# A hybrid decoder step on one core: follow-up steps as streams of their own, decays and heads ahead of the searches, sample values in 128 rows

## The chip, the core and the metric

The kernel runs on one core of a Trainium2 chip. A core has a matrix engine (TensorE, PE in the profile; PEld is its weight load), a vector engine (VectorE, DVE), a scalar engine (ScalarE, ACT), a general engine (GpSimd, POOL) and a queue that issues most transfers (SyncE, SP). Each engine works off its own list of instructions in order; semaphores join them. The metric is the device time of one execution in microseconds (us), as the median of several runs.

## The reference

One layer of a decoder for 1024 prompt tokens and 64 sample tokens (8 sequences of 8), 1088 columns in all, with a model width of 1024:

```python
def token_mixer(x, ...):
    z = split_projection(x @ w_in)              # q_a k_a v_a q_i k_i w_i q_b k_b v_b g_b a_b gate_a gate_b
    attn = attend(q_a, k_a, v_a, q_i, k_i, z['w_i'])   # top 256 keys by an indexer, then softmax
    log_a = log_sigmoid(z['a_b'] @ w_alpha2 + b_alpha) / GATE_TAU
    o_b, s_new = gla_chunked(q_b, k_b, v_b, log_a, gla_s0, gla_chunk)
    o_b = o_b * rsqrt(mean(o_b * o_b) + eps) * gla_norm_g * silu(z['g_b'])
    merged = sigmoid(gate_a) * (attn @ w_attn_o) + sigmoid(gate_b) * (o_b @ w_gla_o)
    return merged @ w_out, k_a, v_a, k_i, s_new

def gla_chunked(...):    # per chunk, 4 heads, key width 128, value width 256
    q_t, k_t = qx * exp(cum), kx * exp(-cum)
    o = tril(q_t @ k_t.T) @ vx + q_t @ s
    s = exp(last) * s + (kx * exp(last - cum)).T @ vx

h = layer_norm(ALPHA * x + mix_out);  y = layer_norm(ALPHA * h + square(relu(h @ w_ff1)) @ w_ff2)
```

The indexer scores every key for every query (`relu(q_i k_i)`, weighted by `w_i`) and keeps the 256 best. For samples the keys are 4096 cached ones, spread over pages, and the new ones.

## The kernel before

Weights and activations are split into a high and a low part, and every projection runs as three matmuls per block of 128 inputs (high x high, low x high, high x low) over columns 0 to 384, 384 to 768 and 768 to 1088. `front` computes everything up to the merged branches and the output projection; `back` does the layer norms and the MLP (`pf`, about 40% of the matmul time).

**What sets the order.** The program is written out once, by a planner. A `Clock` keeps an estimated time for each engine, for each tile the time at which it is ready, and for buffers the time at which they come free. Steps of the work are generators, `Stream`s in a list; a generator yields the tiles that it needs next. `Order.run` takes the first stream of the list whose needs are met by the estimated time of PE (or, if none is, the one whose needs are met first) and lets it issue up to its next yield. So an earlier place in the list is a higher priority, and all steps between two yields go to the engines' lists together. `Engine` passes every instruction through one line, L256, which is why all rows of the profile name that line; they are told apart by their tiles.

**The streams that matter here.**
- `main` runs the jobs, one per block of 128 output columns: `misc` (small projections), `qi`, `ka`, `qa`, `qb`/`kb`, `vb` (`psv`), `gb` (the output gate of GLA), `gate`, then `pmb` (GLA output), `pma` (attention output) and `pwo`. `w_split` makes the high part `wh` of a weight on ACT and the low part `wl` on POOL or DVE.
- `top_first` and `top_second` search the threshold of the prompt's top 256 bit by bit (32 counting steps), on DVE (`ga`) and ACT with DVE (`gb`). Then `fin` turns each tile of scores into a mask (`gta`, `gtb`, `msk`).
- `top_sample` does the same for the samples: in each of 32 steps ACT counts over two halves (`jka`), PE adds the counts (`ppr`), DVE takes the bit (`gs_m`, `gs_u`) and sets the next threshold (`gs_f`).
- `decays` makes the decay factors of a GLA head (`psa`, `cu`, `ge`), `heads` runs the recurrence: `gla` goes through 8 chunks of 128 tokens and, in `sample`, updates the sample states (`pus`, `us`, `gst`) with sample values as a high part `gvh` (128 rows, the values twice) and a low part `gvl` (64 rows), while the keys `gkz` hold high and low parts in rows 0 to 63 and 64 to 127.
- `idx_prompt` and `idx_sample` score the keys (`rh`, `rl`); gathers `cig` fetch the cached indexer keys on POOL's queue.
- `at_soft` and `at_pv` are the attention: scores `psq`, weights `pp`, transposes `ppt`, their high and low parts `phl`, the product `pov`, the output `ao`/`ahl`, stored to `at_s`.
- `ob_load` and `ob_split` fetch the GLA output `ob_s` again as `obl` (eight blocks, first columns 0 to 384, then the other 704) and split it into `obh` and `obl`, which `pmb` multiplies. `gate_job` stores gates to `ga_s` and `gt_load` fetches them as `mgt`.
- `ln_last`, in `back`, is the layer norm of the last columns: sums over eight tiles on PE (`plv`, `pld`), then mean, root and reciprocal on columns of `lr`.

Of the kernel before, what the change touches and what calls it, by code (L numbers as in the profile page):

```python
# [23 lines left out]
P = 128  # L24
# [25 lines left out]
NSH = 6  # L50
# [9 lines left out]
NAHL = 4  # L60
# [314 lines left out]
def front(ph, tc, env, A, O):  # L375
# [37 lines left out]

    def scale_rows(x, r):
# [25 lines left out]
    def w_split(i):  # L440
        for n, e in enumerate(wt[i]):
# [4 lines left out]
            sub(l, r, f32(h), WLATE if 1 < state["job"] < mix_at - 1 else 0.0)  # L446
            e[0], e[1] = h, l

    state = {"dma": 0, "split": 0, "job": 0}

    def w_get(i):
# [6 lines left out]
        hs, ls = [], []  # L458
        for h, l, kn in wt.pop(i):
            for k in range(kn):  # L460
                hs.append(h[:, k, :])
                ls.append(l[:, k, :])
# [182 lines left out]
    def to_stacks(ps, c, st):  # L645
# [5 lines left out]
        for e in range(2):  # L651
            own, oth = slice(e * 64, e * 64 + 64), slice(64 - e * 64, 128 - e * 64)
            dve.tensor_sub(st[e][oth, c0:c0 + n], ps[own, :n], f32(st[e][own, c0:c0 + n]))
# [4 lines left out]
    def qi_job(f):  # L658
        def run(w):
            st = [page(f"qi{2 * f + e}", F32R) for e in range(2)]  # L660
            for c in range(3):
                ps = yield from fmajor(w, c, f"qi{f}_{c}")
                to_stacks(ps, c, st)
# [31 lines left out]
    def qa_job(f):  # L695
        def run(w):
            st = [page(f"qa{2 * f + e}", F32R) for e in range(2)]
            for c in range(3):
                ps = yield from fmajor(w, c, f"qa{f}_{c}")
                to_stacks(ps, c, st)  # L700
# [55 lines left out]
    def idx_sample():  # L756
# [30 lines left out]
        def chunk(p, kh, kl, n):  # L787
# [7 lines left out]
            dve.scalar_tensor_tensor(rl[:, :n], ps[:, :n], 0.0, f32(rh[:, :n]), op0=OP.max, op1=OP.subtract)  # L795
            return rh, rl

        def sums(p, r, n, po, first, last):
            rh, rl = r
# [4 lines left out]
        for qq in range(4):  # L804
            po = [bank("po0", True), bank("po1", True)]
            pend = None
            for p in range(4):
# [7 lines left out]
                for e in range(2):  # L815
# [3 lines left out]
                    if pend:  # L819
                        yield [pend[1][1]]  # L820
                        sums(*pend)
                    pend = (p, r, 512, po[e], p == 0, p == 3)
            yield [pend[1][1]]
# [8 lines left out]
        for p in range(4):  # L832
            r = chunk(p, kkn[:, 0], kkn[:, 1], 64)
            yield [r[1][:, :64]]
# [140 lines left out]
    def masks(g, qts, gte):  # L975
        for i, grp in enumerate(MKP if not mk else ()):
# [207 lines left out]
    def gla(h):  # L1184
# [17 lines left out]
        dve.tensor_sub(vl[:TS], vs[:TS], f32(vh[:TS]))  # L1202
        qz = small("gqz", 512).rearrange("p (a b) -> p a b", b=TS)
# [8 lines left out]
        def sample():  # L1212
# [4 lines left out]
            for i in range(2):  # L1217
# [8 lines left out]
                for j in range(2):  # L1226
                    yield [kz, vh, vl[:TS]]
                    pu = bank("pus")
                    for x in range(2):
                        pe.matmul(pu[:, x * 256:(x + 1) * 256], kz[:, 2 * j + x, :], vh, start=True, stop=False)  # L1230
                        pe.matmul(pu[:, x * 256:(x + 1) * 256], kz[:TS, 2 * j + x, :], vl[:TS], start=False, stop=True)
                    for x in range(2):
                        b = 2 * j + x
                        la = g["lasts"][:, 4 * i + b:4 * i + b + 1]
                        u = small("us", 256)
# [6 lines left out]
            act.activation(vs[:TS], po[:TS, :256], AF.Copy)  # L1242

# [21 lines left out]
        for ci in range(8):  # L1265
# [20 lines left out]
            else:  # L1286
                S2 = small("S", 256)
                dve.scalar_tensor_tensor(S2, S, g["last"][:, ci:ci + 1], u, op0=OP.mult, op1=OP.add)
                S = S2
            if ci < 7:  # L1290
                Sm = small("Sm", 256)
                act.activation(Sm, S, AF.Copy, scale=g["mid"][:, ci + 1:ci + 2])
# [26 lines left out]

    def g_job(h, j):  # L1320
        def run(w):
# [3 lines left out]
            for c in range(3):  # L1325
                c0, n = CH[c]
                pg = yield from fmajor(w, c, f"gb{h}{j}_{c}")
                t = small("gt")
# [53 lines left out]
    def at_soft():  # L1382
# [7 lines left out]
        def norm(x):  # L1390
            rc = tiny("rc", 1)
            dve.reciprocal(rc, x[3][:, 3:4])
            scale_rows(x[2][:, :(x[0][0] + 1) * P], rc)
# [6 lines left out]
        for i, (qt, hp) in enumerate(units):  # L1400
# [11 lines left out]
            for h in range(2):  # L1412
# [18 lines left out]
                if len(fly) > 2:  # L1431
                    yield [fly[0][3][:, 3:4]]
                    norm(fly.popleft())
            if i == len(units) - 1:
                yield [fly[-1][3][:, 2:3]]
                expo(fly[-1])
                while fly:
                    yield [fly[0][3][:, 3:4]]
                    norm(fly.popleft())

    def at_pv():
        tails = deque()

        def tail(qt, hp, po):
# [4 lines left out]
            act.activation(t[:64], po[64:128], AF.Copy)  # L1449
            dve.tensor_tensor(o[:64], po[0:64], t[:64], op=OP.add)  # L1450
# [3 lines left out]
            act.activation(hl[0:64], o[:64], AF.Copy)  # L1454
            sub(hl[64:128], o[:64], f32(hl[0:64]))
            yield [hl]
            c, x0 = qt // 3, (qt % 3) * P
            for e in range(2):
                sp.dma_start(view(f32(at_s[c]), 2 * hp * 64 * 768 + e * 384 + x0, [[768, 64], [64 * 768, 2], [1, P]]),
                             f32(hl[e * 64:e * 64 + 64].rearrange("p (h q) -> p h q", q=P)))  # L1460

# [6 lines left out]
        for _ in units:  # L1468
# [11 lines left out]
            for kt in range(0, qt + 1, 2):  # L1480
# [11 lines left out]
                if len(pend) > 1:  # L1492
                    yield [pend[0][2]]
                    flush(*pend.popleft(), False)
# [5 lines left out]
            while pend:  # L1500
                yield [pend[0][2]]
                flush(*pend.popleft(), not pend)
# [52 lines left out]
    def ob_load():  # L1555
        yield lambda: state["job"] >= merge_at - OBLEAD
# [192 lines left out]
def back(ph, tc, env, A, O):  # L1749
# [114 lines left out]
    def ln(c, z, s, gi, emit, tag):  # L1864
# [28 lines left out]
        r3 = clock.take(pgs.tile([P, 4], F32, name="lr", tag="r3", bufs=2), "lr", "r3", 2)  # L1893
# [633 lines left out]
```

## Time and profile before

| | us |
|---|---|
| median of 3 runs (lowest to highest) | 2090.97 (2090.45 to 2092.82) |
| profiled execution, its own time | 2094.44 |
| its span | 2092.7 |
| PE busy | 2039.7 (97%) |
| DVE busy | 1261.8 (60%) |
| ACT busy | 1121.3 (54%) |
| POOL busy | 774.9 (37%) |
| mean granted clock of PE | 0.987 |

Times in rows of the profile are from the start of the span. Matmuls are pipelined: a row's duration is longer than the distance to the next start, so it is the distance that a matmul costs. A wait is put down to the semaphore that came last.

### The profile page before, as it was taken

The page shows a single profiled execution, that of the slowest core. Times are in us where ns is not written, and L with a number is a line of the kernel's source. Part 1 is how long each engine was busy: PE and PEld are TensorE (multiplying, and loading weights), DVE is VectorE, ACT ScalarE, POOL GpSimd, SP SyncE. Part 2 cuts the span into 40 slices and gives each one's busy share as a digit, 9 for nine tenths or more (in the row PEclk, how much of TensorE's full clock was granted, in tenths as well). Part 3 has the DMA queues.
Part 4 walks back from the last instruction along what each step waited for, and adds up shares of the span by engine and source line. Part 5 has one row for each costly group of instructions (what it writes and reads, how often), then busy time and mean ns, then how long its engine had stood idle before and what let it go on. Part 6 is the DMA issues. An engine that isn't in the chain of part 4 may idle for free.

```text
span 2092.7 us, 34594 instructions
## 1 busy us (share of the span) xinstructions
PE 2039.7 (97%) x12443; PEld 1965.4 (94%) x12443; DVE 1261.8 (60%) x2630; ACT 1121.3 (54%) x2222; POOL 774.9 (37%) x579
## 2 busy tenths in 40 slices
PE   7999999999799999999999999999999999999998
PEld 7989999898789999999999899999899999999997
DVE  6976776756845666753167844565654453566635
ACT  5678777787567765674023424455353242445543
POOL 3344121212221113113134324565655343354455
PEclk9999999999899999999999999999999999999998
DMA  6664301212023224245473234655533343235542
GB/s 237 260 188 140 124 21 51 95 34 92 23 72 127 83 83 139 84 135 196 170 277 121 71 89 130 188 155 166 148 100 111 122 130 107 66 129 163 186 151 89
DMA packets 185596, 264.51 MB, mean 126 GB/s; under 512 B 22208, under 2 KB 119488, under 8 KB 185424
## 3 DMA queue, kind: packets, MB, share of 16 engines
q1 hardware_dynamic: 177872, 236.87, 35.1%
q0 software_dynamic: 7552, 25.43, 3.9%
q8 instruction: 98, 1.61, 0.3%
q14 instruction: 74, 0.61, 0.1%
HBM read 212.72 MB, written 49.51 MB: 125 GB/s over the span
## 4 chain that ended last, share of the span: by engine, by line
PE 87%; DVE 5%; issue 4%; POOL 2%; ACT 2%; DMA 1%; SPq 0%; ACTq 0%; POOLq 0%; DVEq 0%
PE pf L256 32%; PE gate L256 9%; PE gb L256 5%; PE pwo L256 4%; PE psv L256 4%; PE pmb L256 4%; PE qb L256 2%; PE kb L256 2%; PE qa L256 2%; PE po L256 2%; PE qi L256 2%; PE psc L256 2%; PE pma L256 2%; PE psq L256 2%; PE pov L256 2%
## 5 line engine op out<-in xcount | busy, mean ns | idle before, releaser
L256 PE MATMUL pf<-a,w 128*128 128x384 f32 (+1 forms) x2304 | 397.4, 328 | 2.3 <-POOL a L256 1.3
L256 PE MATMUL pf<-h,w 128*128 128x384 f32 (+1 forms) x2304 | 396.4, 329 | 3.0 <-POOL w L256 1.7
L256 PEld LDWEIGHTS pf<-h,w 128*128 128x128 f32 x2304 | 380.9, 189 | 5.6 <-POOL w L256 2.1
L256 PEld LDWEIGHTS pf<-a,w 128*128 128x128 f32 x2304 | 378.4, 188 | 6.6 <-POOL a L256 1.8
L256 POOL TENSOR_TENSOR wl<-wr,wh 128x1024 fp32r<-128x1024 f32 (+1 forms) x66 | 150.6, 2283 | 470.0 <-ACT wh L256 415.1
L256 POOL TENSOR_TENSOR w<-wr,w 128x512 fp32r<-128x512 f32 x142 | 202.2, 1433 | 130.6 <-ACT w L256 122.0
L256 ACT ACTIVATE w<-wr 128x512 fp32r<-128x512 f32 x272 | 156.5, 618 | 62.2 <-PE pwo L256 25.8
L256 DVE TENSOR_TENSOR w<-wr,w 128x512 fp32r<-128x512 f32 x130 | 135.0, 1046 | 52.7 <-ACT w L256 52.4
L256 DVE TENSOR_TENSOR acc<-acc,pf 128x384 f32<-128x384 f32 (+1 forms) x136 | 72.9, 538 | 94.9 <-PE pf L256 92.9
L256 PE MATMUL gate<-xh,wh 128*128 128x384 f32 (+1 forms) x384 | 129.9, 338 | 0.0
L256 PE MATMUL gate<-xh,wl 128*128 128x384 f32 (+1 forms) x384 | 125.5, 327 | 0.0
L256 PE MATMUL gate<-xl,wh 128*128 128x384 f32 (+1 forms) x384 | 125.4, 327 | 0.0
L256 POOL TENSOR_TENSOR a<-fr,a 128x384 fp32r<-128x384 f32 (+1 forms) x54 | 52.6, 974 | 195.0 <-ACT a L256 188.5
L256 ACT ACTIVATE wh<-wr 128x1024 fp32r<-128x1024 f32 (+1 forms) x75 | 74.4, 1006 | 76.2 <-DMA wr<-wgo 39.4
L256 DVE TENSOR_TENSOR fr<-fr,pf 128x384 f32<-128x384 f32 (+1 forms) x96 | 50.8, 529 | 91.8 <-ACT fr L256 91.5
L256 ACT ACTIVATE fr<-pf 128x384 f32<-128x384 f32 (+1 forms) x96 | 44.9, 467 | 114.2 <-PE pf L256 112.7
L256 ACT ACTIVATE a<-fr 128x384 fp32r<-128x384 f32 (+1 forms) x96 | 48.7, 507 | 81.1 <-DVE fr L256 79.1
L256 DVE TENSOR_SCALAR_CACHE_REDUCE jk<-sc,ga_f 128x1024 int8<-128x1024 f32 (+2 forms) x96 | 88.4, 921 | 2.1
L256 ACT ACTIVATE jkb<-sc,gb_f 128x896 int8<-128x896 f32 (+2 forms) x96 | 86.0, 896 | 4.4 <-DVE gb_f L256 2.7
L256 DVE TENSOR_TENSOR phl<-ppt,phl 128x512 fp32r<-128x512 f32 (+1 forms) x80 | 50.2, 637 | 60.4 <-ACT phl L256 59.9
L256 PE MATMUL psv<-wh,xh 128*128 128x256 f32 (+1 forms) x288 | 83.8, 291 | 0.0
L256 PE MATMUL psv<-wl,xh 128*128 128x256 f32 (+1 forms) x288 | 81.2, 282 | 0.0
(507 smaller groups left out, 5182.9 us busy)
## 6 DMA issues: line engine op xcount, KB each, us to landing
wr<-wff SPq DMA_DIRECT2D x256, 256.0 KB
wr<-w SPq DMA_DIRECT2D x43, 512.0 KB
ckr<-kT SPq DMA_DIRECT2D x256, 64.0 KB
ga_s<-gate SPq DMA_DIRECT2D x16, 544.0 KB
ci_s<-cig SPq DMA_DIRECT2D x16, 512.0 KB
kir<-ci_s SPq DMA_DIRECT2D x16, 512.0 KB
wr<-wout SPq DMA_DIRECT2D x13, 512.0 KB
mgp<-ga_s SPq DMA_DIRECT2D x16, 384.0 KB
```

The source lines that it names most:

```text
L256: r = f(*a, **k)
```

## The change

- **Order of the streams.** `decays` and `heads` stand ahead of the searches `top_second`, `top_first` and of `later` in the list (before: behind them, `heads` first).
- **Follow-ups as streams (`task`).** A step that waits for the result of another engine and was issued with it (the low half of a weight, of the index queries, of the relu scores and of the attention weights; the update of the sample state and its store; the gating of the GLA output and its store) becomes a stream at the head of the list, which issues when its input is ready by the clock. `force` issues it at once where its result is needed. PSUM banks are held for them (`pinned`), and `room` waits for a free buffer.
- **Sample values.** `gvl` is filled up with zeros on POOL to 128 rows, and the second `pus` matmul of a pair multiplies all 128.
- **Smaller ones.** 7 buffers for small tiles in place of 6 (`NSH`), 3 for `ahl` in place of 4 (`NAHL`); `ob_load` begins only when all 24 pieces of the GLA output were stored; `ln_last` sums seven of the eight tiles in a bank of their own (`plw`) ahead of the last one and takes the reciprocal right behind the root.

The core of the diff:

```diff
+    def task(gen):
+        live[:] = [x for x in live if not x.done]
+        live.append(order.add(gen, engines=(), at=len(live)))
+        return gen
+    def force(gen):
+        for _ in gen:
+            pass
...
             act.activation(h, r, AF.Copy)
-            sub(l, r, f32(h), WLATE if 1 < state["job"] < mix_at - 1 else 0.0)
+            owed.setdefault(i, []).append(task(w_low(l, r, h)))
...
         dve.tensor_sub(vl[:TS], vs[:TS], f32(vh[:TS]))
+        pool.memset(f32(vl[TS:]), 0.0)
...
-                        pe.matmul(pu[:, x * 256:(x + 1) * 256], kz[:TS, 2 * j + x, :], vl[:TS], start=False, stop=True)
+                        pe.matmul(pu[:, x * 256:(x + 1) * 256], kz[:, 2 * j + x, :], vl, start=False, stop=True)
...
                         act.activation(u, pu[:, x * 256:(x + 1) * 256], AF.Copy, scale=la)
-                        dve.scalar_tensor_tensor(st[i][:, b, :], st[i][:, b, :], la, u, op0=OP.mult, op1=OP.add)
-                sp.dma_start(O["gla_s"][4 * i:4 * i + 4, h].rearrange("b k v -> k b v"), st[i])
+                        us.append((u, st[i][:, b, :], la))
+                    unpin(pu)
+                    task(update(us, O["gla_s"][4 * i:4 * i + 4, h].rearrange("b k v -> k b v") if j else None, st[i]))
...
                 act.activation(hl[:, 0, :256 * m], pt, AF.Copy)
-                dve.tensor_sub(hl[:, 1, :256 * m], pt, f32(hl[:, 0, :256 * m]))
-                pend.append((kt, m, hl))
+                clock.pinned.add(pt.tensor.name)
+                pend.append((kt, m, hl, task(low(hl, pt, m))))
...
-        yield lambda: state["job"] >= merge_at - OBLEAD
+        yield lambda: state["job"] >= merge_at - OBLEAD and outs[0] == 24
...
+    order.add(decays(), margin=M_GL)
+    s_gl = order.add(heads(), margin=M_GL)
     s_tq = order.add(top_second(), engines=("act",), slack=1.0)
     s_tp = order.add(top_first(), engines=("dve",), slack=1.0)
     s_la = order.add(later(), engines=("dve",), slack=0.5)
-    s_gl = order.add(heads(), margin=M_GL)
-    order.add(decays(), margin=M_GL)
...
             if f == 6:
-                pool.tensor_tensor(sd, sd, z[6], op=OP.add)
-                yield [s2, sd]
+                dve.tensor_tensor(sd, sd, z[6], op=OP.add)
+                yield [sd]
                 pe.matmul(pd[:, :n], on, sd, start=True, stop=False)
+                cols(pw, 3, sd)
+                yield [s2]
+                cols(pw, 0, s2)
+                yield [pw[:, :6]]
...
         act.activation(r3[:, :3], v3[:, :3], AF.Sqrt, bias=eps)
+        yield [r3[:, :3]]
+        dve.reciprocal(r3[:, :3], r3[:, :3])
         ds = small("lds")[:, :n]
         act.activation(ds, pd[:, :n], AF.Copy)
-        dve.tensor_tensor(z[0], z[0], pd[:, :n], op=OP.subtract)
-        dve.reciprocal(r3[:, :3], r3[:, :3])
```

How it moves instructions, at three places. First DVE where the last mask of the prompt's second search is made (`gtb` its flags, `sc` its scores, `msk` the mask) and the sample search takes its bit from the sums `ppr`. Before, with the 15th of the 34 `gs_m`:

```order
L256 SCALAR_TENSOR_TENSOR gtb<-sc_430,cg,gtb 128x768
L256 SCALAR_TENSOR_TENSOR msk_5338<-gtb 128x768
L256 TENSOR_SCALAR gtb,cg<-sc_432,gb_u 128x512
L256 TENSOR_SCALAR gtb<-sc_432,gb_u 128x512
L256 TENSOR_SCALAR cg<-cg 128x1
L256 SCALAR_TENSOR_TENSOR sc_432<-one,gtb 128x512
L256 SCALAR_TENSOR_TENSOR gtb<-sc_432,cg,gtb 128x512
L256 SCALAR_TENSOR_TENSOR msk_5339<-gtb 128x512
L256 TENSOR_SCALAR gs_m<-ppr 128x1
L256 COPY_PREDICATED gs_u<-gs_m,gs_f 128x1
L256 TENSOR_SCALAR gs_f<-gs_u 128x1
L256 TENSOR_TENSOR cu<-cu,ge 128x1088
```

Now, with the 14th:

```order
L256 TENSOR_SCALAR gtb<-sc_443,gb_u 128x512
L256 TENSOR_SCALAR cg<-cg 128x1
L256 SCALAR_TENSOR_TENSOR sc_443<-one,gtb 128x512
L256 SCALAR_TENSOR_TENSOR gtb<-sc_443,cg,gtb 128x512
L256 SCALAR_TENSOR_TENSOR msk_4567<-gtb 128x512
L256 TENSOR_SCALAR cu<-psa,b_al 128x384
L256 TENSOR_SCALAR gs_m<-ppr 128x1
L256 COPY_PREDICATED gs_u<-gs_m,gs_f 128x1
L256 TENSOR_SCALAR gs_f<-gs_u 128x1
L256 TENSOR_SCALAR cu<-psa,b_al 128x384
```

The masks have moved one search step forward, and other work of the heads (`cu`) stands behind them. On PE, 129 rows stood from the 14th to the 16th `ppr` before; now 271 stand between the 13th and the 14th.

Second PE and SP at the end of the attention. On PE, before, the attention's last steps stood by themselves ahead of `pmb`:

```order
L256 MATMUL pov<-phl,vpr_8637 128x256 x4
L256 MATMUL psq<-kar_8635,qq_10149 128x128
L256 MATMUL psq<-kar_8636,qq_10149 128x128
L256 MATMUL ppt<-idf,pp 128x128 x4
L256 MATMUL pov<-phl,vpr_8637 128x256 x4
L256 MATMUL ppt<-idf,pp 128x128 x2
L256 MATMUL pov<-phl,vpr_8637 128x256 x2
L256 MATMUL ppt<-idf,pp 128x128 x2
L256 MATMUL pmb<-obh_10333,wh_0_10049 128x384
L256 MATMUL pmb<-obl_10061,wh_0_10049 128x384
```

Now its last `pov` stands among the matmuls of the last gate:

```order
L256 MATMUL gate_2_10349<-xh_116,wl_0_9941 128x320
L256 MATMUL gate_2_10349<-xh_117,wh_0_9940 128x320
L256 MATMUL gate_2_10349<-xl_125,wh_0_9940 128x320
L256 MATMUL gate_2_10349<-xh_117,wl_0_9941 128x320
L256 MATMUL pov<-phl,vpr_8521 128x256 x2
L256 MATMUL gate_2_10349<-xh_118,wh_0_9940 128x320
L256 MATMUL gate_2_10349<-xl_126,wh_0_9940 128x320
L256 MATMUL gate_2_10349<-xh_118,wl_0_9941 128x320
```

Fifteen more gate rows and then `pmb` follow. On SP at the same place, before (a row's last part names what it waits for: DMAHW are the eight semaphores of earlier transfers, the others are engines):

```order
L256 DMA at_s_84<-ahl 64x2x128 [waits DMAHW1_49,Pool_49]
L256 DMA obl_10061<-ob_s_75 128x704 [waits DMAHW2_49]
L256 DMA obl_10063<-ob_s_76 128x704 [waits DMAHW3_49]
L256 DMA obl_10065<-ob_s_77 128x704 [waits DMAHW4_49]
L256 DMA ga_s_93<-gate_10053 128x1088 [waits DMAHW5_49,Activation_49]
L256 DMA mgt<-ga_s_86 128x1088 [waits DMAHW6_49,DVE_49]
L256 DMA mgt<-ga_s_87 128x1088 [waits DMAHW7_49,PE_49]
L256 DMA at_s_83<-ahl 64x2x128 [waits DMAHW0_49]
L256 DMA at_s_83<-ahl 64x2x128 [waits DMAHW1_49,Pool_49]
L256 DMA obl_10067<-ob_s_78 128x704 [waits DMAHW2_49]
```

Now:

```order
L256 DMA at_s_83<-ahl 64x2x128 [waits DMAHW1_49,Pool_49]
L256 DMA ga_s_93<-gate_10214 128x1088 [waits DMAHW2_49,Activation_49]
L256 DMA mgt<-ga_s_86 128x1088 [waits DMAHW3_49,PE_49]
L256 DMA mgt<-ga_s_87 128x1088 [waits DMAHW4_49,PE_49]
L256 DMA obl_10357<-ob_s_81 128x384 [waits DMAHW5_49]
L256 DMA obl_10400<-ob_s_82 128x384 [waits DMAHW6_49]
L256 DMA at_s_83<-ahl 64x2x128 [waits DMAHW7_49]
L256 DMA at_s_83<-ahl 64x2x128 [waits DMAHW0_49,Pool_49]
L256 DMA obl_10223<-ob_s_75 128x704 [waits DMAHW1_49]
L256 DMA obl_10225<-ob_s_76 128x704 [waits DMAHW2_49]
L256 DMA obl_10227<-ob_s_77 128x704 [waits DMAHW3_49]
```

Eleven of the sixteen `obl` loads stood ahead of the last store of a gate (`ga_s`) and of the two `mgt` loads; now six do, and all eight of the long ones stand behind.

Third POOL at the start (`cig` the gathers of indexer keys, `wl` the low half of a weight). Before:

```order
L256 TENSOR_TENSOR wl_0_184<-wr_0_114,wh_0_183 128x1024
L256 MEMSET hsel 128x128
L256 AFFINE_SELECT hsel<-hsel 128x128
L256 IOTA cb_238 128x64
L256 IOTA cq_240 128x64
L256 IOTA cb_252 128x8
L256 DMA cig_256<-ciT,ix_i 128x1024
L256 DMA cig_258<-ciT,ix_i 128x1024
L256 MEMSET as_268 64x1088
L256 TENSOR_TENSOR wl_0_391<-wr_0_280,wh_0_390 128x1024
```

Now:

```order
L256 DMA cig_255<-ciT,ix_i 128x1024
L256 DMA cig_257<-ciT,ix_i 128x1024
L256 MEMSET as_267 64x1088
L256 TENSOR_TENSOR wl_0_184<-wr_0_114,wh_0_183 128x1024
L256 DMA cig_293<-ciT,ix_i 128x1024
L256 DMA cig_296<-ciT,ix_i 128x1024
L256 DMA cig_344<-ciT,ix_i 128x1024
L256 DMA cig_353<-ciT,ix_i 128x1024
L256 DMA cig_377<-ciT,ix_i 128x1024
L256 TENSOR_TENSOR wl_0_282<-wr_0_140,wh_0_281 128x1024
```

The first two gathers moved ahead of the first low half, and five more stand ahead of the second one on POOL.

More of the change, by code (lines that the diff above doesn't have):

```diff
@@ L49 @@
 NSM = 6
-NSH = 6
+NSH = 7
 KAHEAD = 2
@@ L412, in sub, with room @@
             dve.tensor_sub(out, a, b)
+    live = []
+    def task(gen):
+        live[:] = [x for x in live if not x.done]
+        live.append(order.add(gen, engines=(), at=len(live)))
+        return gen
+    def room(tag, n):
+        return lambda: not clock.uses or len(clock.free.get(tag, range(99))) >= n
+    def force(gen):
+        for _ in gen:
+            pass
     def scale_rows(x, r):
@@ L650, in to_stacks, with low @@
             act.activation(st[e][own, c0:c0 + n], ps[own, :n], AF.Copy)
-        for e in range(2):
-            own, oth = slice(e * 64, e * 64 + 64), slice(64 - e * 64, 128 - e * 64)
-            dve.tensor_sub(st[e][oth, c0:c0 + n], ps[own, :n], f32(st[e][own, c0:c0 + n]))
+        clock.pinned.add(ps.tensor.name)
+        def low():
+            for e in range(2):
+                own, oth = slice(e * 64, e * 64 + 64), slice(64 - e * 64, 128 - e * 64)
+                yield [f32(st[e][own, c0:c0 + n])]
+                dve.tensor_sub(st[e][oth, c0:c0 + n], ps[own, :n], f32(st[e][own, c0:c0 + n]))
+            unpin(ps)
+        return task(low())
     qis = {}
@@ L794, in chunk, with low @@
             act.activation(rh[:, :n], ps[:, :n], AF.Relu)
-            dve.scalar_tensor_tensor(rl[:, :n], ps[:, :n], 0.0, f32(rh[:, :n]), op0=OP.max, op1=OP.subtract)
-            return rh, rl
+            clock.pinned.add(ps.tensor.name)
+            def low():
+                yield [f32(rh[:, :n])]
+                dve.scalar_tensor_tensor(rl[:, :n], ps[:, :n], 0.0, f32(rh[:, :n]), op0=OP.max, op1=OP.subtract)
+                unpin(ps)
+            return rh, rl, task(low())
         def sums(p, r, n, po, first, last):
-            rh, rl = r
+            rh, rl = r[:2]
             w = wsel[:, p].rearrange("p e b -> p (e b)")
@@ L1242, in sample, with update @@
             act.activation(vs[:TS], po[:TS, :256], AF.Copy)
+        def update(us, out, t):
+            for u, x, la in us:
+                yield [u]
+                dve.scalar_tensor_tensor(x, x, la, u, op0=OP.mult, op1=OP.add)
+            if out is not None:
+                sp.dma_start(out, t)
         def quads(i):
@@ L1438, in at_soft @@
                     yield [fly[0][3][:, 3:4]]
-                    norm(fly.popleft())
+                    yield from norm(fly.popleft())
     def at_pv():
@@ L1892, in ln @@
         yield [pv[:, :3]]
-        r3 = clock.take(pgs.tile([P, 4], F32, name="lr", tag="r3", bufs=2), "lr", "r3", 2)
+        r3 = clock.take(pgs.tile([P, 8], F32, name="lr", tag="r3", bufs=2), "lr", "r3", 2)
         act.activation(r3[:, :3], pv[:, :3], AF.Sqrt, bias=eps)
@@ L1936, in ln_last, with cols @@
         s2, sd = small("ls2")[:, :n], small("lsd")[:, :n]
-        pv, pd = bank("plv", True), bank("pld", True)
+        pv, pw, pd = bank("plv", True), bank("plw", True), bank("pld", True)
+        def cols(p, i, x):
+            for j, o in enumerate(off):
+                pe.matmul(p[:, i + j:i + j + 1], x[:, o:o + P], on[:, :1], start=True, stop=True)
         for f in range(8):
@@ L1950, in ln_last @@
             if f == 6:
-                pool.tensor_tensor(sd, sd, z[6], op=OP.add)
-                yield [s2, sd]
+                dve.tensor_tensor(sd, sd, z[6], op=OP.add)
+                yield [sd]
                 pe.matmul(pd[:, :n], on, sd, start=True, stop=False)
+                cols(pw, 3, sd)
+                yield [s2]
+                cols(pw, 0, s2)
+                yield [pw[:, :6]]
+                r3, v3 = (clock.take(pgs.tile([P, 8], F32, name="lr", tag="r3", bufs=2), "lr", "r3", 2) for _ in range(2))
+                dve.tensor_copy(v3[:, :6], pw[:, :6])
+                unpin(pw)
         yield [q]
-        for j, o in enumerate(off):
-            for i, (x, y) in enumerate(((s2, q), (sd, z[7]))):
-                pe.matmul(pv[:, 3 * i + j:3 * i + j + 1], x[:, o:o + P], on[:, :1], start=True, stop=False)
-                pe.matmul(pv[:, 3 * i + j:3 * i + j + 1], y[:, o:o + P], on[:, :1], start=False, stop=True)
+        cols(pv, 3, z[7])
+        cols(pv, 0, q)
         pe.matmul(pd[:, :n], on, z[7], start=False, stop=True)
```

72 lines of the change are left out of this document (55 added, 17 removed).

## Prediction

> **What bounds the kernel now.** I read the head of the profile page first, then the list of what TensorE (PE) waited for, then windows of the span, and last the timelines around the places that these name.
>
> ```profile
> span 2092.7 us, 34594 instructions
> PE 2039.7 (97%) x12443; PEld 1965.4 (94%) x12443; DVE 1261.8 (60%) x2630; ACT 1121.3 (54%) x2222; POOL 774.9 (37%) x579
> PE 87%; DVE 5%; issue 4%; POOL 2%; ACT 2%; DMA 1%; SPq 0%; ACTq 0%; POOLq 0%; DVEq 0%
> ```
>
> PE is busy for 97% of the span and carries 87% of the chain that ended last. Only two things can therefore change the time: matmuls that take less PE time, or gaps between matmuls. The profiled execution took 2094.44 us (the span and 1.7 us around it), 3.5 us more than the 2090.97 us median. I sum against 2094.44 and take 3.5 off at the end.
>
> ```profile
> PE ppr L256 <- ACT jka L256: 11.5, 2, 8.6
> PE pov L256 <- ACT phl L256: 4.6, 2, 2.7
> PE plr L256 <- DVE lr L256: 1.2, 1, 1.2
> PE pld L256 <- POOL lsd L256: 0.9, 1, 0.9
> ```
>
> Each row gives who waited, for whom, then the total us, the number of waits and the longest. Two waits of `ppr` (the sum over both halves of the sample keys in a search step) and two of `pov` (attention times V) are the largest that the change can reach. The next windows give, after the stretch, the busy us and instruction counts of PE, PEld, DVE, ACT and POOL, then the granted clock, the DMA share and GB/s.
>
> ```profile
> 560.00:576.00 16.00, 7.44 (x32) 7.08 (x31) 15.43 (x20) 4.95 (x10) 10.76 (x9) 0.70 0.00 0
> 938.00:962.00 24.00, 18.91 (x94) 17.45 (x92) 18.51 (x47) 18.66 (x51) 9.15 (x6) 0.79 0.64 208
> ```
>
> In the first PE runs 32 matmuls in 16 us while DVE is full. In the second, 94 matmuls fill 24 us at a granted clock of 0.79.
>
> **Part 1: sample values in 128 rows.** The low half `gvl` gets 64 more rows, filled with zeros, so that the second matmul of each `pus` pair covers 128 rows like the first.
>
> ```profile
> 312.03 0.47 PE L256 MATMUL pus<-gvh,gkz 128*128 128x256 f32 x1
> 312.43 0.38 PE L256 MATMUL pus<-gvl,gkz 64*128 64x256 f32 x1
> 312.74 0.39 PE L256 MATMUL pus<-gvh,gkz 128*128 128x256 f32 x1
> 313.05 0.38 PE L256 MATMUL pus<-gvl,gkz 64*128 64x256 f32 x1
> 313.36 0.41 PE L256 MATMUL kb<-xh,wh 128*128 128x320 f32 x1
> ...
> 952.40 0.41 PE L256 MATMUL pov<-phl,vpr 128*128 128x256 f32 x2
> 952.64 0.34 PE L256 MATMUL pmb<-obh,wh 128*128 128x384 f32 x1
> ```
>
> The first column is the start; matmuls overlap, so the cost is the distance between starts. A group of four takes 313.36 - 312.03 = 1.33 us, 0.31 to 0.40 each. Two `pov` matmuls of the same width, type and 128 rows take 0.24 us, 0.12 each. The group should then cost 4 x 0.12 = 0.48, a saving of 0.85 us. There are 16 groups (4 heads, 2 halves of the batch, 2 pairs): 13.6 us. I take 12.8 (0.8 each), since a part of the 0.40 at the front is the entry from other work. Bounds: if only the 64-row matmuls drop to 0.12, 32 x 0.19 = 6.1 us; if the matmul behind each group gains 0.1 us too, 15.2. The rows do not exclude zero, if it is the fresh weights of each matmul and not their rows that cost; that is rival E. Four memsets of 64x256 are added on POOL, about 0.25 us each by the 64x1088 one that is shown under part 4 (1.02 us); POOL is busy for 37% and hides them.
>
> The Trainium skill, "TensorE: Matmul & The Clock Gate", section "Why this matters for your kernels", says that a single matmul over few rows takes the same time as one over 128; by that the term would be 0 and the sum 2080.5. The page "TensorEngine Tiling (Array Packing)", section "Key Properties", says that a change of tiling mode drains TensorE, which would fit 0.31 beside 0.12. The rows side with the second, so I keep the term.
>
> **Part 2: decays and heads ahead of the searches; follow-ups as streams.** The streams are served in list order, and many DVE, POOL and SP steps leave their generator and are issued when their input is there. That moves instructions on every engine. The search first:
>
> ```profile
> 540.21 0.28 PE L256 MATMUL ppr<-gs_p,pm 128*128 128x2 f32 x2
> 554.87 0.38 PE L256 MATMUL ppr<-gs_p,pm 128*128 128x2 f32 x2 [2.92 <-ACT jka L256]
> 556.08 0.52 PE L256 MATMUL gb<-xh,wl 128*128 128x384 f32 x1
> 556.40 0.52 PE L256 MATMUL gb<-xh,wh 128*128 128x384 f32 x1
> ...
> 560.24 0.33 PE L256 MATMUL gb<-xh,wl 128*128 128x384 f32 x1
> 560.41 0.33 PE L256 MATMUL gb<-xh,wh 128*128 128x384 f32 x1
> 571.04 0.59 PE L256 MATMUL ppr<-gs_p,pm 128*128 128x2 f32 x2 [8.56 <-ACT jka L256]
> ```
> ```profile
> 552.17 1.15 DVE L256 TENSOR_SCALAR_CACHE_REDUCE gtb<-sc,gb_u 128x896 int8<-128x896 f32 x1
> 567.61 0.22 DVE L256 TENSOR_SCALAR gs_m<-ppr 128x1 int32<-128x1 f32 x1
> ```
> ```profile
> 568.42 1.15 ACT L256 ACTIVATE jka<-ssa,gs_f 128x1024 int8<-128x1024 f32 x1 [9.07 <-DVE gs_f L256]
> 570.81 0.19 ACT L256 ACTIVATION_READ_ACCUMULATOR jka<-ssb,gs_f 128x1 f32 x1
> ```
>
> These are the 14th, 15th and 16th `ppr`. The answer to the 15th, `gs_m`, stands on DVE behind the whole mask finishing of the prompt search (`gtb`, `msk`), which runs from 552.17 to 567.61; `jka` counts after that, and the 16th `ppr` waits 8.56 us, with the rest of PE's queue behind it. After each gap a matmul takes 0.32 us (556.08 to 556.40), not 0.17 (560.24 to 560.41): the granted clock is halved. About 10 matmuls after the first wait and 16 after the second run so, at 0.15 us lost each, 4 us; with 11.5 of waits 15.5. Before, 97 PE instructions lay between the 14th and 15th `ppr` and 32 between the 15th and 16th, 129 against some 27 us of DVE work (540.21 to 567.61). Now the masks stand between the 13th and 14th `gs_m`, 45 DVE instructions in place of 43, and 271 PE instructions between those two `ppr`: at 0.12 to 0.17 us each 32 to 46 us, more than the 27. I take -15, with 0 (another stall of that kind elsewhere) and -15.5 as ends.
>
> **Part 3: the end of attention.** There PE now runs the last gate matmuls between the last `pov`, so the `pov` waits should go. The window of 938 to 962 holds 94 matmuls: about 77 of `pmb` at 0.17 and 17 of `pov` and `ppt` at 0.12 are 15 us; 24 - 15 = 9 us were lost. But the same new order puts SP's loads of `obl`, which `pmb` needs, elsewhere.
>
> ```profile
> 938.87 0.32 SPq L256 DMA_DIRECT2D ga_s<-gate  x1
> 939.28 1.24 SPq L256 DMA_DIRECT2D mgt<-ga_s  x2
> 942.67 1.84 SPq L256 DMA_DIRECT2D obl<-ob_s  x3
> ```
> ```profile
> ga_s<-gate SPq DMA_DIRECT2D x16, 544.0 KB
> obl<-ob_s SPq DMA_DIRECT2D x8, 352.0 KB
> ```
> ```profile
> 944.00:946.00 2.00, 0.29 (x1) 0.29 (x1) 1.12 (x3) 1.92 (x6) 0.00 (x0) 0.50 0.99 312
> ```
> ```profile
> 1.28 0.42 SPq L256 DMA_DIRECT2D ptg<-page_rows  x1
> ```
> ```profile
> 4.15 0.66 DVE L256 TENSOR_SCALAR ix_i<-ptg 128x2 int32<-128x2 int32 x8 [2.05 <-DMA ptg<-page_rows]
> ```
>
> Before, eleven of the sixteen `obl` loads were issued ahead of the last `ga_s<-gate`. Now two short ones (192 KB) and all eight long ones (352 KB) stand behind it, and behind two `mgt` loads of the same 544 KB. SP's queue keeps its order, and the store waits for the last gate matmul (call its end T). Bytes from T on: 3 x 0.557 + 2 x 0.197 + 8 x 0.360 = 4.95 MB; at the 312 GB/s of the row (DMA share 0.99) 15.9 us. From T to the first byte I take 3 us, an estimate: a load of 1 KB at the start is issued at 1.28 and used at 4.15, 2.9 us later. So the last long load lands at T + 19. The matmuls over columns 384 to 768 end about 1.3 us later and the last 24 (0.15 each) at T + 24; dense, the job of 72 matmuls would take 11.9. So about 12 us are lost where 9 were: +2.5 (12 - 9, less some overlap). Ends: no wait at all, -9; a rate of 250 GB/s, +6.
>
> **Part 4: the start, and the end.**
>
> ```profile
> 17.00:20.00 3.00, 3.00 (x19) 3.00 (x18) 2.53 (x6) 1.17 (x3) 0.00 (x0) 1.00 1.03 393
> ```
> ```profile
> 12.16 1.23 POOL L256 DMA_INDIRECT cig<-ciT,ix_i  x1 [0.19 <-issue]
> 15.00 1.02 POOL L256 MEMSET as<- 64x1088 f32 x1
> ```
> ```profile
> 2083.23 0.17 DVE L256 RECIPROCAL lr<-lr 128x3 f32<-128x3 f32 x1
> 2085.14 3.76 DVE L256 SCALAR_TENSOR_TENSOR acc<-acc,lnp,plr 128x320 f32<-128x320 f32 x8 [0.17 <-PE plr L256]
> ```
>
> At the start two index gathers now go ahead of the first low half of the weights on POOL and five more ahead of the second, where two were issued in all before 30 us. They are 512 KB each into a stretch where the DMA already moves 393 GB/s: up to 3 x 0.52 / 0.393 = 4 us more for the last pieces of x, partly covered. I take +1.5 (0 to +3). At the end the sums over seven of the eight tiles are made before the last matmuls, `lsd` is added on DVE (the 0.9 us wait goes), and the reciprocal follows its root directly rather than behind the subtraction; of the 1.9 us from 2083.23 to 2085.14 one subtraction stays. -1.5 (-0.8 to -1.6).
>
> **The rest of the order.** Some 900 us are replanned, and a wait that I did not find may arise: +2, between 0 and +10 (as much as the two `ppr` waits). The second half of the program (`back`) keeps its order up to its last layer norm, so it gives nothing. One more buffer for small tiles and one fewer for `ahl` cost nothing beside that order.
>
> Sum: -12.8 - 15 + 2.5 + 1.5 - 1.5 + 2 = -23.3; 2094.44 - 23.3 = 2071.1; less 3.5 gives 2067.6. Forecast: **2068 us**.
>
> **Rivals.**
> - B, the loads are hidden anyway: if the DMA delivers in time, the 9 us are kept, 11.5 better than my term, 2056. For it: 393 GB/s is possible. Against: the row at 944 shows 312 with a share of 0.99.
> - C, the search stall comes back elsewhere: the masks still take 15 us of DVE at a stretch, and a heads' follow-up or a low half behind them could stop PE. If 12 of the 15 us return, 2080.
> - E, the 64 rows are not the cause: the term of part 1 is 0, 2080.5. Against it stand 0.31 and 0.12 us at the same width.
> - D, slower: every search step becomes PE's wait. A step needs the count from 568.42 to 571.00, 2.6 us, and some 1.2 us for `gs_m` to `gs_f` and `ppr`: 3.8 us if nothing stands ahead of it on DVE and ACT. Now that heads and decays come first, more does. The shortest distance between two `ppr` is now 33 PE instructions, about 5 us, so from 1.2 us of queue on PE waits. It ends slower if the 34 steps lose 0.8 us each on average, 27 us: 2095. Against it: before, two steps of 34 waited, and the mean distance was as long (65 instructions then, 64 now).
>
> **How the numbers follow.** Forecast 0.50 (2060 to 2076), B 0.14, C 0.20, E 0.06, D 0.10. The range must leave out no more than 0.2: it drops D, the low half of B and the top of C, 2057 to 2087. A difference under 0.2% (4.2 us) cannot be told from none. Faster than 2086.8 are the forecast, B, E and two thirds of C: 0.83. The rest of C lies within 0.2%: 0.07. D gives slower: 0.10.
>
> **What the profile after would show.** Part 1: `pus` starts about 0.12 us apart, no 64x256 form. Part 2: no `ppr` wait for `jka` above 1 us and no half clock between 500 and 600 us. Part 3: `pov` off the list of waits, and behind the last `gate` matmul a wait of `pmb` for `obl`, with the DMA near 300 GB/s and about 12 us lost; if B holds, nothing there. Part 4: the last `misc` matmuls 1 to 3 us later, the last `acc` work 1.5 us shorter. The forecast is wrong if a wait of over 8 us stands at another place, or if `pus` keeps 0.3 us.

## The result, and the profile after

The changed kernel takes 2067.74 us (median of 4 runs, 2066.76 to 2068.22), the kernel before 2091.64 us (4 runs): 0.9885 of it, with a 95% interval of 0.9868 to 0.9902. The forecast was 2068 us. The profiled execution took 2067.98 us with a span of 2066.3, 26.5 us less than the profiled one before.

The head of the page, and what PE waited for (us in total, times, longest):

```profile
span 2066.3 us, 34576 instructions
PE 2020.5 (98%) x12443; PEld 1953.1 (95%) x12443; DVE 1267.4 (61%) x2634; ACT 1112.9 (54%) x2215; POOL 781.9 (38%) x587
```
```profile
PE misc L256 <- ACT wh L256: 8.8, 1, 8.8
PE pmb L256 <- ACT obh L256: 5.2, 1, 5.2
PE misc L256 <- ACT xh L256: 3.6, 3, 1.7
PE pwo L256 <- DVE mg L256: 3.5, 4, 2.6
...
PE plr L256 <- DVE lr L256: 0.5, 1, 0.5
```

The two `ppr` waits are gone from the list, and the two of `pov` for ACT (one of `pov` for DVE, 0.8 us, is left). New are a wait of `pmb` for the high half of `obl`, and three of `misc` for x. The granted clock is 1.00 where it was 0.86 on average, as the window of 550 to 600 us shows, first before, then after (PE, PEld, DVE, ACT, POOL busy, granted clock, DMA share, GB/s):

```profile
550.00:600.00 50.00, 38.51 (x207) 34.96 (x205) 35.46 (x59) 28.92 (x60) 21.09 (x14) 0.86 0.15 47
```
```profile
550.00:600.00 50.00, 50.00 (x298) 45.00 (x298) 21.41 (x47) 37.98 (x89) 10.51 (x8) 1.00 0.22 72
```

298 matmuls in place of 207 fit into these 50 us. A group of sample-state matmuls, on PE's timeline after:

```profile
295.57 0.47 PE L256 MATMUL pus<-gvh,gkz 128*128 128x256 f32 x1
295.88 0.28 PE L256 MATMUL pus<-gvl,gkz 128*128 128x256 f32 x1
296.00 0.28 PE L256 MATMUL pus<-gvh,gkz 128*128 128x256 f32 x1
296.12 0.28 PE L256 MATMUL pus<-gvl,gkz 128*128 128x256 f32 x1
296.23 0.59 PE L256 MATMUL po<-Sm,gq 128*128 128x256 f32 x2
```

The starts lie 0.12 us apart where they lay 0.31 apart. Only the first costs 0.31, the entry from the matmuls ahead of it. The group takes 0.66 us in place of 1.2 to 1.3. Eight of the 16 groups now stand in pairs, so that the entry is paid twelve times.

The end of the attention, on the timelines of PE, SP and ACT:

```profile
913.05 0.31 PE L256 MATMUL gate<-xh,wl 128*128 128x320 f32 x1
...
916.24 0.34 PE L256 MATMUL pmb<-obh,wl 128*128 128x384 f32 x1
921.76 0.69 PE L256 MATMUL pmb<-obh,wh 128*128 128x384 f32 x1 [5.19 <-ACT obh L256]
```
```profile
913.86 0.33 SPq L256 DMA_DIRECT2D ga_s<-gate  x1
914.28 1.28 SPq L256 DMA_DIRECT2D mgt<-ga_s  x2
915.61 1.01 SPq L256 DMA_DIRECT2D obl<-ob_s  x2
...
918.02 4.90 SPq L256 DMA_DIRECT2D obl<-ob_s  x8
```
```profile
921.18 0.98 ACT L256 ACTIVATE obh<-obl 128x384 fp32r<-128x384 f32 x2 [6.11 <-DMA obl<-ob_s]
```

PE runs the gate and the first six blocks of `pmb` without a gap and then stands until the seventh block has come through the queue behind the gate store and the two `mgt` loads. The DMA ran at the rate of the forecast while the gate store, the `mgt` loads and two `at_s` stores were in the queue, and faster than forecast once only loads were left:

```profile
915.00:917.00 2.00, 1.57 (x9) 1.24 (x8) 0.77 (x2) 0.07 (x1) 0.00 (x0) 1.00 1.02 309
917.00:919.00 2.00, 0.00 (x0) 0.00 (x0) 0.00 (x0) 0.00 (x0) 0.00 (x0) 1.00 0.92 311
...
921.00:925.00 4.00, 3.24 (x9) 2.76 (x10) 1.68 (x3) 2.29 (x5) 1.00 (x1) 0.50 1.05 411
925.00:929.00 4.00, 3.89 (x16) 3.33 (x16) 2.70 (x6) 2.35 (x5) 0.00 (x0) 0.78 1.04 407
```

### The profile page after: what moved, and what is told of

It reads as the page before. It is cut to its first block, busy times and chain, and to the rows that moved or that the text cites. A ratio compares the mean times of both kernels' runs of the same rounds, so it can differ in the third digit from the quotient of the medians.

```text
span 2066.3 us, 34576 instructions
## 1 busy us (share of the span) xinstructions
PE 2020.5 (98%) x12443; PEld 1953.1 (95%) x12443; DVE 1267.4 (61%) x2634; ACT 1112.9 (54%) x2215; POOL 781.9 (38%) x587
## 4 chain that ended last, share of the span: by engine, by line
PE 86%; DVE 5%; issue 4%; DMA 2%; ACT 2%; POOL 1%; SPq 0%; ACTq 0%; POOLq 0%; DVEq 0%
PE pf L256 33%; PE gate L256 8%; PE gb L256 4%; PE pmb L256 4%; PE pwo L256 4%; PE psv L256 4%; PE qb L256 2%; PE kb L256 2%; PE qa L256 2%; PE po L256 2%; PE psc L256 2%; PE pma L256 2%; PE pov L256 2%; PE psq L256 2%; PE qi L256 2%
## 5 line engine op out<-in xcount | busy, mean ns | idle before, releaser
L256 DVE CUSTOM_DVE_ANT_0 pp<-psq,msk 128x512 f32<-128x512 f32 (+3 forms) x96 | 51.4, 553 | 54.0 <-PE psq L256 50.6
```

The source lines that it names most:

```text
L256: r = f(*a, **k)
```

## The experiments

Each is told with its median, and its ratio to the kernel before, measured on the same chip in the same session. The kernel before was run in all four sessions (medians 2091.64, 2093.07, 2093.38 and 2090.99 us), the changed kernel in the first alone. A difference between an experiment and the changed kernel therefore compares two sessions, and is good to about 2 us. "Lost" below means the time between starts of successive matmuls beyond the median distance of matmuls of the same shape in that kernel, summed over a stretch of the trace of one execution.

**rows64: the rows alone, undone.**

```diff
-  pe.matmul(pu[:, x * 256:(x + 1) * 256], kz[:, 2 * j + x, :], vl, start=False, stop=True)
+  pe.matmul(pu[:, x * 256:(x + 1) * 256], kz[:TS, 2 * j + x, :], vl[:TS], start=False, stop=True)
```

> The changed kernel with one thing undone: the second matmul of each pus pair covers 64 rows again (the zeros are still written, and every engine keeps its order). First theory: the 64 rows cost, on their own matmul and on the 128-row one behind it, so the 16 groups go back from about 0.5 to about 1.3 us each: 13 us slower than the changed kernel, about 2081 us, with starts 0.31 apart in each group. Rival: fresh weights and not rows cost, then 2068 us. Second rival: only the 64-row matmuls cost, then 6 us, 2074.

Measured: 2080.47 us (2079.25 to 2081.56), 0.9943 (0.9927 to 0.9958), 12.7 us more than the changed kernel (12.1 by the two ratios). Starts on PE's timeline:

```profile
307.19 0.47 PE L256 MATMUL pus<-gvh,gkz 128*128 128x256 f32 x1
307.59 0.38 PE L256 MATMUL pus<-gvl,gkz 64*128 64x256 f32 x1
307.90 0.38 PE L256 MATMUL pus<-gvh,gkz 128*128 128x256 f32 x1
308.21 0.38 PE L256 MATMUL pus<-gvl,gkz 64*128 64x256 f32 x1
```

The 128-row matmul behind a 64-row one costs 0.31 us too (307.90 to 308.21), with weights as fresh as in the changed kernel, where it costs 0.12. So the 64 rows cost, on their own matmul and on the 128-row one behind it; rival E falls, and so does the half price. By the traces the 64 `pus` matmuls take 20.7 us here and 9.5 in the changed kernel, and the matmuls behind the groups add 1.1: 12.3 us, near the 12.7 of the medians. That the change between 64 and 128 rows is the whole cost is not shown. Two other 64-row matmuls of the same shape in a row (`pob`), in the changed kernel, are 0.22 us apart, where 128-row ones are 0.12 apart:

```profile
1353.07 0.50 PE L256 MATMUL pob<-v_n,ptl 64*128 64x256 f32 x2
1353.50 0.81 PE L256 MATMUL pf<-a,w 128*128 128x384 f32 x3
```

**before_rows128: the rows alone, done.**

```diff
+  nc.gpsimd.memset(f32(vl[TS:]), 0.0)
-  pe.matmul(pu[:, x * 256:(x + 1) * 256], kz[:TS, 2 * j + x, :], vl[:TS], start=False, stop=True)
+  pe.matmul(pu[:, x * 256:(x + 1) * 256], kz[:, 2 * j + x, :], vl, start=False, stop=True)
```

> The kernel before with the zero rows and the 128-row matmul alone, every engine in its old order. If the gain of the rows stands by itself: 2091.6 - 13 = 2078.6 us. Rival: DVE sets the end of the two ppr waits near 555 and 571 us, so that the PE time saved ahead of them is waited for there; then the ppr waits grow from 11.5 to 16 us or more and the time falls by 3 to 8 us only, 2084 to 2088.

Measured: 2083.74 us (2080.75 to 2086.6), 0.9959 (0.9945 to 0.9972): 6 to 11 us less than before, between the two cases. The profiled execution was the fastest of the five, 2080.75, and in it the `ppr` waits have not grown:

```profile
PE ppr L256 <- ACT jka L256: 11.7, 2, 8.8
```

The rival is therefore not what its trace shows: there the time falls by 13.7 us against the profiled execution before, 12.4 at the `pus` groups and 1.4 ahead of the first `psi`, where both kernels have the same order. The other runs fell by less; this kernel and the one before spread over 6 to 8 us from run to run in that session, the changed one over 1.5 in its own. Where runs of the two kernels have the same mean granted clock they differ by about 12 us (at 0.986, 2083.7 and 2083.8 against 2095.1 and 2095.7; at 0.988, 2080.8 against 2092.4 to 2093.1). But this kernel's clock was lower on the whole, 0.984 to 0.989 against 0.986 to 0.990, and why stays open.

**list_only: the order of the streams alone.**

```diff
+    order.add(decays(), margin=M_GL)
+    s_gl = order.add(heads(), margin=M_GL)
     s_tq = order.add(top_second(), engines=("act",), slack=1.0)
     s_tp = order.add(top_first(), engines=("dve",), slack=1.0)
     s_la = order.add(later(), engines=("dve",), slack=0.5)
-    s_gl = order.add(heads(), margin=M_GL)
-    order.add(decays(), margin=M_GL)
```

> The kernel before with the list order alone: decays and heads ahead of the searches, no follow-up streams, 64 rows. The order that comes out has the prompt's masks behind the 20th gs_m with 111 PE instructions after the next ppr, but the searches end 480 PE instructions later, so that 141 PE instructions of attention stand alone behind the last gate. First theory: the list order needs the follow-ups, and by itself the ppr waits go (-15) while the end of the attention loses some 30 us in its place: about 2108 us (2095 to 2125). Rival: the list order is what removed the ppr waits, and most of the gain is there: 2078.

Measured: 2142.64 us (2139.04 to 2145.19), 1.0238 (1.0222 to 1.0253), 49 us slower. That is the direction of the first theory, but 18 us beyond the end of its range. What PE waited for:

```profile
PE gate L256 <- POOL wl L256: 14.6, 1, 14.6
PE pov L256 <- ACT phl L256: 13.7, 14, 1.7
PE pov L256 <- DVE phl L256: 9.7, 18, 1.5
```

Of the 11.5 us of `ppr` waiting for `jka` 1.1 are left, but the searches end so late that the attention stands alone behind the gates: 47.6 us are lost from the last gate matmul to the first `pma` (10.8 before). And a low half on POOL stands where it holds PE up for 14.6 us.

**follow_ups_only: the changed kernel with the old order of the streams.** The edit is the diff above, turned round, in the changed kernel.

> The changed kernel with decays and heads behind the searches again (follow-ups as streams and 128 rows stay). The prompt's masks now stand behind the 9th gs_m with 120 PE instructions to the next ppr and 31 to the one after, some 23 us of PE work against 25 us of DVE work. First theory: a ppr wait of 2 to 6 us comes back there, half clock included 3 to 9; of the obl loads 6 stand behind the last gate store in place of 10, which gives back 2 to 4: about 2070 us (2066 to 2076). Rival: the searches ahead of the heads bring the whole stall of 15 us back: 2083. Second rival: the follow-ups alone carry the gain: 2064.

Measured: 2086.47 us (2085.3 to 2088.05, five runs; a sixth, of 5536.62, is left out), 0.9966 (0.9953 to 0.9979), 18.7 us more than the changed kernel. That is nearer to the rival's 2083 than to the 2070 of the first theory, but what comes back is not at `ppr`. PE's and DVE's timelines:

```profile
473.28 0.49 PE L256 MATMUL pot<-idf,gv 128*128 128x128 f32 x3
486.19 0.69 PE L256 MATMUL gb<-xh,wh 128*128 128x384 f32 x1 [12.42 <-DVE gt L256]
```
```profile
470.16 1.15 DVE L256 TENSOR_SCALAR_CACHE_REDUCE gtb<-sc,gb_u 128x896 int8<-128x896 f32 x1
...
484.98 0.69 DVE L256 SCALAR_TENSOR_TENSOR msk<-gtb 128x512 bf16<-128x512 int8 x1
485.59 0.55 DVE L256 SCALAR_TENSOR_TENSOR gt<-gt,gb 128x384 f32<-128x384 f32 x1
```

The same masks, 470.16 to 485.6 on DVE in one piece, now stand ahead of `gt`, the gating of the GLA output, and PE's `gb` waits for the bank that `gt` has to read.

**Masks held to DVE's time: three kernels.** In each, one line ahead of the masks of the second search:

```diff
+        s_tq.engines = ("dve",)
         yield from masks(g, ACT_SEARCH, page("gtb", I8, [P, 4 * T]))
```

In follow_ups_masks_paced:

> The changed kernel with the old list order (2087.03), with the masks held to DVE's time: behind the 9th, 10th and 11th gs_m. First theory: its waits of gb for gt (12.4 us) and of psas for gk (5.3 us) are the same masks standing ahead of other DVE work: they go, but for 2 to 4 us, 2087 - 15 = 2072. Rival: with the searches ahead of the heads DVE is behind at that place by more than the masks, and 10 us or more of waits stay: 2080 or more.

Measured: 2074.35 us, 0.9922 (0.9905 to 0.9940), 12.1 us less than without the line (9 by the two ratios). The wait for `gt` is down to about 1 us and that of `psas` is still there, so it was not the masks':

```profile
450.50 0.45 PE L256 MATMUL psas<-gq,gk 128*64 128x64 f32 x2 [5.27 <-DVE gk L256]
480.25 0.55 PE L256 MATMUL pot<-idf,gv 128*128 128x128 f32 x3 [0.73 <-DVE gs_m L256]
481.81 0.48 PE L256 MATMUL gb<-xh,wh 128*128 128x320 f32 x1 [1.01 <-DVE gt L256]
```

In before_masks_paced:

> The kernel before with one line: while the second search makes its masks, its stream is held to DVE's estimated time instead of ACT's, so that the three masks come behind the 17th, 18th and 19th gs_m in place of all behind the 14th. No list order, no follow-up streams, 64 rows. First theory: the ppr waits of 11.5 us and their half clock are these masks in one piece; they go (to under 2 us), 2093 - 15 = 2078, plus up to 6 at the end of the attention, whose last 43 PE instructions now stand behind the last gate: 2078 to 2084. Rival: DVE has too much work there whatever the order, so that another wait (gt, S or gst on DVE) takes the place: 2090 or more.

Measured: 2097.24 us (2095.25 to 2099.49), 1.0028 (1.0018 to 1.0038): 6 us slower, where the first theory had 7 to 13 less. What PE waited for:

```profile
PE pov L256 <- ACT phl L256: 7.6, 7, 1.7
...
PE ppr L256 <- ACT jka L256: 2.9, 1, 2.9
PE pmb L256 <- DVE obl L256: 2.8, 4, 2.2
```

The 8.6 us wait of `ppr` is gone, and from 540 to 580 us 5.3 us are lost in place of 16.1; so it was the masks. The first one, of 2.9, has stayed: in the kernel before, ACT's list has the copy of the last `psv` ahead of `jka`,

```profile
551.98 0.38 ACT L256 ACTIVATE gvs<-psv 64x256 f32<-64x256 f32 x1 [2.13 <-PE psv L256]
552.26 1.14 ACT L256 ACTIVATE jka<-ssa,gs_f 128x1024 int8<-128x1024 f32 x1
```

so `jka` waits for PE's last `psv`, and the `ppr` that stands behind it on PE waits for `jka`. And what was won is lost again at the end of the attention, whose last steps stand behind the gates here (21.6 us lost from the last gate to `pma`, 10.8 before). The theory had allowed 6 us for that. Where the rest of the 6 us went is not shown.

In obl_early_masks_paced (the earlier `obl` loads of the next experiment as well):

> The kernel with the earlier obl loads (2059.15), with the masks held to DVE's time as well: behind the 15th, 16th and 17th gs_m. First theory: the masks cost PE nothing there any more, 2059, between 2057 and 2061. Rival: the 45 DVE instructions in one piece still cost a us or two elsewhere: 2056.

Measured: 2059.8 us (2059.26 to 2061.12), 0.9852 (0.9835 to 0.9869), as without the line (2059.15): where PE has other work in its list, the masks in one piece cost nothing that these runs can show.

**obl_early: the loads of obl one gate job earlier.**

```diff
-OBLEAD = 1
+OBLEAD = 2
```

> The changed kernel with the loads of obl allowed one gate job earlier (OBLEAD 2), so that all sixteen stand ahead of the last store of a gate on SP. First theory: the 11 us lost between the last gate matmul and the first pma are the transfers behind that store; they go, but for 1 to 3 us at the end of the attention: 2067.7 - 9, about 2059 us (2056 to 2062). Rival: the splitting of obl on ACT and DVE or the halved clock costs as much, then 2065 or more. Second rival: the earlier pages for obl take room from the attention, and pov waits return, then 2067 or more.

Measured: 2059.15 us (2058.77 to 2059.88), 0.9838 (0.9823 to 0.9854): 8.6 us less than the changed kernel (9.8 by the two ratios), and the lowest median of all. All `obl` loads now stand ahead of the last gate store on SP, and from 900 to 1010 us PE waits for one thing only:

```profile
PE ppt L256 <- ACT pp L256: 0.6, 1, 0.6
```

From the last gate to `pma` 0.2 us are lost in place of 11.1. From `pma` to `pf`, in the output projection (`pwo`), 1.3 us more are lost; that stretch has one order in all thirteen kernels and loses 6.0 to 9.7 us, so this may be chance.

**low_at_once and obl_first_low: the start.** The low halves of the first two weights (of the first alone, together with the earlier loads) are issued with their high halves:

```diff
-            owed.setdefault(i, []).append(task(w_low(l, r, h)))
+            t = task(w_low(l, r, h))
+            if i < 2:          # i < 1 in the second
+                force(t)
+            owed.setdefault(i, []).append(t)
```

> The changed kernel with the low halves of the first two weights issued together with their high halves, so that the index gathers stand behind the first low half on POOL's queue again and four fewer of them share the DMA with x. First theory: the waits of misc for xh (3.6 us) go, and 2 to 2.5 us stay gained: 2065.5. Rival: later gathers make the index scores (psi, pss) later by as much, since the two kernels stood level again at the first psi, 49.7 us before and 49.0 after: 2067.7, no change.

> The changed kernel with the loads of obl one gate job earlier (which gave 2059.15) and the low half of the very first weight alone issued at once, so that the gathers stand behind it but the second low half keeps its new place. First theory: the misc waits for xh go (2 to 4 us) and psi keeps its order, since the qi steps are not moved: 2056.5 (2055 to 2058). Rival: as with the first two weights, psi waits for qi and r and takes back more than the 3 us: 2062 to 2066.

Measured: 2076.1 us (2074.81 to 2078.49) for the first, 0.9924 (0.9911 to 0.9936), 8.4 more than the changed kernel, which neither theory had; 2059.66 (2057.53 to 2060.95), 0.9835 (0.9822 to 0.9849), for the second, as without the edit, 2059.15, and below its rival's range. In the first the waits of `misc` for x go, as expected (8.9 us lost up to the first `psi`, 12.6 in the changed kernel), but from `psi`, the index scores, to the first `va` 8.4 us more are lost:

```profile
PE psi L256 <- DVE qi L256: 3.5, 2, 2.8
PE psi L256 <- ACT r L256: 1.6, 1, 1.6
```

The edit also moved DVE's work on the page indices ahead of the last low halves of `qi`. In the second 2.8 us are won ahead of `psi` and 5.1 lost behind it, against the kernel with the earlier loads. Up to the first `psi` the seven kernels that share the order of the changed one there lose 12.3 to 12.7 us, the four with the order before 8.7 to 10.2. So the early gathers cost 2 to 4 us at their place, and these edits do not win that back.

**old_norm_end: the last layer norm as before**, the part of the diff in `ln_last` turned round.

> The changed kernel with the last layer norm (ln_last) as before: lsd added on POOL, all sums of columns after the last matmul, the reciprocal behind a subtraction. First theory: 1.5 to 2 us slower, 2069.5, all of it after the last pf matmul (11.5 to 13 us there in place of 10). Rival: the last waits are on the way of the output only, 2067.7.

Measured: 2068.22 us (2068.04 to 2069.7), 0.9880 (0.9865 to 0.9895), 0.5 us more, which cannot be told from none. Behind the last `pf` 4.0 us are lost in place of 1.9, with the old waits back (PE's timeline):

```profile
2051.87 0.81 PE L256 MATMUL pld<-lsd,on 128*128 128x320 f32 x2 [0.91 <-POOL lsd L256]
...
2057.41 1.65 PE L256 MATMUL plr<-idf,lr 128*128 128x128 f32 x6 [1.19 <-DVE lr L256]
```

The place itself can be read from all the traces. From the start of the last `pf` to the end of the span the eight kernels with the new end take 14.29 to 14.32 us, the five with the old end 15.85 to 16.42, and this one 16.05: the new end is worth 1.5 to 2.1 us. The medians hide a part of that: this execution lost 1.2 us less in `pwo` than the changed kernel, in the same order of instructions.

## Why the prediction was right, and where it was not

| step | predicted, us | measured, us | by |
|---|---|---|---|
| 1, sample values in 128 rows | -12.8 | -12.4 | `pus` matmuls and those behind them, before and after (rows64: 12.3 by the traces, 12.7 by the medians) |
| 2, `ppr` waits and half clock | -15 | about -14.7 | 27.1 won from the first `qb` to the last gate, less the 12.4 |
| 3, end of attention and `obl` | +2.5 | +0.2 | lost from last gate to `pma`, 10.8 and 11.1 |
| 4, start | +1.5 | +2.4, then -3.0 | lost to the first `psi`, and from there to the first `qb` |
| 4, end | -1.5 | -1.9 | lost behind the last `pf` |
| the rest | +2 | +2.9 | what is left of the 26.5; 2.3 of it lost from `pma` to `pf` |

- **Step 1** came out at nearly its size, 0.8 us for each of 16 groups, but its parts were other: about 0.7 us in the group, whose entry still costs 0.31 us with 128 rows, and the rest in the matmul behind it, which the step had kept for its upper bound.
- **Step 2** is right in its sum and, for about 11 of the 16 us lost there, in its cause: the masks in one piece on DVE, with too little PE work in the list beside them. before_masks_paced takes the long wait away with one line. The short wait, which the step put to the same account, came from ACT's list; in the changed kernel it is gone, and what took it away was not tested alone. That the list order or the follow-ups alone would bring this gain was not claimed, and neither does: list_only is 49 us slower, and follow_ups_only puts the masks before another step. It is where the masks land among PE's work that pays.
- **Step 3** was right in its mechanism, which decided between the forecast and rival B: the `pov` waits go and the transfers behind the gate store take their place, nearly one for one; obl_early shows the 8.6 us that the hidden loads of B would have given. The size was off on both sides. The forecast of 12 us lost was for the 72 matmuls of the first `pmb` job, and these lost 9.4: 5.4 in the wait for the seventh block, 2.6 in matmuls at the half clock behind it, and only 1.4 in waits for the long blocks, since the 312 GB/s held only up to 919 us and the loads behind ran at 407 to 411. And the loss before was 10.8 over the whole stretch from the last gate to the first `pma`, not the 9 of the window that was read.
- **Step 4**: the loss at the start is real, with the misc waits for x that were named, and at the upper end of its 0 to 3 us or above (2.4 against the profiled execution before, up to 4 against other kernels with its order there). What the step left out is that 3.0 us come back by the first `qb`: 5.0 to 5.5 us are lost there in the four kernels without follow-ups, 1.9 to 2.5 in the seven that share the order of the changed kernel up to there. Whether the earlier gathers bring that, or the low halves of the index queries as streams, the runs do not separate. The end came out as forecast.
- **The rest** was where the sum was weakest. `back` was said to give nothing, and between its first and last `pf` it does not (21.3 us lost before, 21.2 after). The 2.3 us from `pma` to `pf` are waits of `pwo` for `mg` that differ from execution to execution: 6.0 to 9.7 us lost in thirteen kernels with one order there. They are no effect of the change that can be shown. The buffer counts and the condition on `ob_load` were not tested alone.
- The agreement of 2067.74 with 2068 is better than the sum deserves, and partly luck. Against the profiled executions the change brought 26.5 us, the sum said 23.3; that the profiled execution before was 3.5 us above its median, which was taken off, made up for it.
- Rival D (every search step a wait) did not come: no `ppr` wait is left. Its reading of the distances was too short: in the trace of the changed kernel at least 39 matmuls and 7.4 us lie between two `ppr`, not 33 and about 5, against the 3.8 us that a step needs. Rival C did not come in the changed kernel, but follow_ups_only is just that rival: the masks stop PE for 12.4 us at another place.

## What to carry to other kernels

When every engine works its list in order, a long piece of work on a side engine costs nothing or most of its length (here 15.4 us of masks cost none, or waits of 8.6 and 12.4), according to what stands behind it there and how much the main engine has in its list meanwhile; count the instructions between the two meeting points before and after. A wait that is removed at the end of a stage can merely uncover the transfers that ran beneath it, so look in the queue that issues them for a store that waits for the stage's last result, and put loads that need nothing from it ahead. Price an operand that fills half the rows by the distance between starts, and pad it with zeros when its neighbours use all rows.

## What the runs showed of the hardware that was not expected

- The 128-row matmul behind a 64-row one is as slow as the 64-row one itself: 0.31 us, where it takes 0.12 between its equals (rows64 and the changed kernel, with the same weights). Two 64-row ones in a row lie 0.22 us apart.
- With loads alone in SP's queue the DMA moved 407 to 411 GB/s at a share of 1.04 to 1.05. With stores and loads mixed it moved 312 GB/s at a share of 0.99 in the kernel before, and 309 to 311 at 0.92 to 1.02 in the changed one. A share near 1 did not mean that this was the highest rate. What in the mix costs the rate is not shown.
